# A trace-time planner gets measured durations, and its bisection steps are queued behind regular work

## The chip, the cores and the metric

The kernel runs on 1 core of one Trainium2 chip. The metric is the device time of one execution in microseconds (us). The engines are PE (TensorE matmul; PEld is its weight load), DVE (VectorE), ACT (ScalarE), POOL (GpSimd) and SP (SyncE, which issues the DMAs). Each engine runs its own instruction stream in order; semaphores order the streams against each other.

## The reference

One step of a one-layer hybrid encoder, in float32, for a prompt of 1024 frames and 8 running streams of 16 frames (128 more rows), so 9 tiles of 128 rows; tile 8 is the samples.

```python
h = rmsnorm(x, norm_mix); proj = h @ w_in           # xr, gate, q, k, v, qi, ki, wi
xc, conv_new = causal_conv(xr, conv_prev, conv_w, conv_b)
hs, h_last = rglru(xc, pos, h_prev, ...)            # h = a*h_prev + b, a scan over time
y_a = hs * gelu(gate)
q = rope(rmsnorm(q, q_norm), pos); k = rope(rmsnorm(k, k_norm), pos)
idx_score = sum_heads(relu(qi @ ki.T) * wi)         # -inf outside the 64-frame chunk mask
sel = top_k(idx_score, topk)                        # 256 of up to 1024 keys; 132 of 528 for a sample
y_b = attention of q over the selected k, v only
x = x + concat([y_a, y_b]) @ w_out
x = x + (silu(gate) * up) @ w_ffn_out               # SwiGLU, D_FF = 2816
```

## The kernel before, in words

Every float32 product is made of three matmuls on a high and a low part of each operand (`mm3`, line 243; its matmuls are line 205). The work runs in stages: keys, values and the first norm; the index scores (`index`, line 622); the RG-LRU (`lru_main`, line 1028, four blocks of 128 channels, each in three time pieces of 384 columns); the q projection (`q_tile`, line 1197, two halves of nine tiles); the first half of `W_out` with the rotation of k and the norm of q (`out_tile`, line 1341; `k_rope`; `q_norm`, line 1224, nine POOL multiplications); attention of prompt tiles 0 to 7 and of the eight samples (`attn`, line 1385); the second half of `W_out`; the feed-forward part (`ffn`, line 1623).

**Names.** In the RG-LRU `xp` is the padded input, `xc` the convolved one (ACT copies of PSUM tiles, with the matmuls of line 210 between them), and `tr`, `ti`, `tt` are the gate tiles that DVE turns into the scan over time (`TENSOR_TENSOR_SCAN tr<-tt,ti`). In the q stage `qn` is the normed query and `rp` the POOL part of its rotation; `to` is a small output tile that DVE copies out just as the stage begins. In attention `m` is a head's scores and `mx` its maximum: DVE adds the mask `s` of a tile to the scores in PSUM and takes the maximum in one instruction (printed `ISA m,mx<-ps,s`); ACT makes the exponential and POOL divides; PE transposes `m` (line 215); DVE makes the low part of the result (`rest` and `smr` are buffers for it).

**Top-k by bisection.** The 256th largest score of each row is found bit by bit (`topk`, line 792), in two groups that run beside the stages (line 769, `TK`). Group 0 holds tiles 2 to 5. One of its 32 steps is four ACT instructions over `s` (sign with a sum, `jk<-s,tk_cand`, 384 to 768 columns), then three small DVE updates of `tk_cand`. Group 1 holds tiles 6, 7 and 8. One of its 32 steps (16 on the upper 16 bits, 16 on the lower) is three DVE instructions with a sum over a 16-bit `key` of 896, 1024 and 528 columns (`jk<-key,tk_cnt`, in the first half `jk<-key,tk_cand`), then two or three small updates; such a step is called a pass below. At its end each group makes its masks (`topk_mask`, line 909): a compare, a prefix sum, a second compare with a sum and a third on DVE, and a sum and a scaling of `s` on POOL. Attention of a tile waits for its mask (line 1391), and the samples' part needs tile 8's.

**What sets the order.** All stages are Python generators ("streams"), which `Kernel.run` (line 93) steps while the program is traced. `run` keeps estimates only: `clock`, `pe` (the work handed to PE) and `busy` for each of DVE, ACT and POOL, the time until which that engine has work. Every call of an engine goes through `Metered` (line 36), which adds `fixed + n * each` to `busy`; all such instructions are recorded as line 66. A stream names the time at which it wants to go on. The bisection groups are `side` streams and "fillers" of one engine (line 316: group 0 of ACT, group 1 of DVE): one is stepped when the clock reaches `busy` of its engine less `SLACKS[phase]` (line 103; phases 0 to 4 are index, RG-LRU, q projection, first half of W_out, attention), or in a gap of the estimate of at least `FILL` before a regular instruction (`fill`, line 137). The resulting program is then ordered once more by the framework's scheduler, which follows priorities; `step` (line 155) lowers a filler's priority by 400 places.

Of the kernel before, what the change touches and what calls it, by code (L numbers as in the profile page):

```python
# [11 lines left out]
BF16 = mybir.dt.bfloat16  # L12
I32 = mybir.dt.int32
I16 = mybir.dt.int16
# [21 lines left out]
class Metered:  # L36


    def __init__(self, engine, kernel, name, fixed, each):
        self.engine, self.kernel, self.name, self.fixed, self.each = engine, kernel, name, fixed, each  # L40

    def __getattr__(self, op):
        f = getattr(self.engine, op)
        if op in ("dma_start", "wait", "semaphore") or not callable(f):
            return f

        def call(*args, **kw):
            n = 1
            for a in args:
                if hasattr(a, "shape") and len(a.shape) > 1:  # L50
                    n = max(n, int(np.prod(a.shape[1:])))
            each = self.each
            if self.name == "vector" and op in ("tensor_copy", "tensor_scalar") and "accum_out" not in kw:
                each *= 0.5
            if self.name == "vector" and kw.get("accum_out") is not None and args[1].dtype in (BF16, I16):
                each *= 0.5
            k = self.kernel
            start = k.now() if k.chain is None else k.chain + k.HOP
            k.fill(self.name, start)
            end = max(k.busy[self.name], start) + self.fixed + n * each  # L60
            if self.name == "scalar" and op == "activation":
                end += k.table(args[2])
            k.busy[self.name] = end
            if k.chain is not None:
                k.chain = end
            return f(*args, **kw)  # L66

        return call


class Engines:
    def __init__(self, nc, kernel):
        self.nc = nc
        for name, fixed, each in (("vector", 0.07, 0.00104), ("scalar", 0.2, 0.00072), ("gpsimd", 0.05, 0.0012)):
            kernel.busy[name] = 0.0
            setattr(self, name, Metered(getattr(nc, name), kernel, name, fixed, each))

    def __getattr__(self, x):
        return getattr(self.nc, x)
# [2 lines left out]
class Kernel:  # L82
    def __init__(self, ctx, tc, I, O):
        self.ctx, self.tc, self.I, self.O = ctx, tc, I, O
        self.pe = self.pe0 = 0.0
        self.clock = 0.0
        self.phase = 0
        self.chain = None
        self.busy, self.filler, self.side, self.gap = {}, {}, [], None
        self.nc = Engines(tc.nc, self)  # L90


    def run(self, streams, width, side=(), carry=()):
# [7 lines left out]
        def due(x):  # L101
            e = self.filler.get(x[1])
            return x[0] if e is None else max(x[0], self.busy[e] - self.SLACKS[self.phase])

# [49 lines left out]

    def step(self, g):

        n = self.LATER.get(self.filler.get(g), 0)
        if not n:
            return next(g, None)
        with self.tc.high_priority(offset=-n):  # L160
            return next(g, None)

    def begin(self):

# [27 lines left out]
    TABLES = {"exp": (AF.Exp, AF.Tanh), "sqrt": (AF.Sqrt,), "gelu": (AF.Gelu_apprx_tanh, AF.Tanh), "silu": (AF.Silu,)}  # L192
    SYNC = 0.3
    HOP = 0.1
    SLACKS = (1.5, 1.5, -3.0, -3.0, 1.5)
    QUEUE = 8.0
    AHEAD = 2.0

# [1 line left out]
    def mm(self, out, lhsT, rhs, start, stop):  # L200
        n = 1
        for v in rhs.shape[1:]:
            n *= v
        self.pe += max(n, 256 if lhsT.shape[-1] > 64 else 128) / 2400.0
        self.nc.tensor.matmul(out, lhsT, rhs, start=start, stop=stop)  # L205

    def mm4(self, out, lhsT, rhs, start, stop):
# [1542 lines left out]
```

## Time and profile before

| | us |
|---|---|
| median of 3 runs | 1586.41 (1585.03 to 1586.87) |
| the profiled execution | 1582.82, of which the span is 1580.7 |
| PE busy | 1477.3 (93%) |
| DVE busy | 886.4 (56%) |
| ACT busy | 624.4 (39%) |
| POOL busy | 288.7 (18%) |

Busy time is that of one engine over the whole span; the stages differ widely. The stages lie in the span about so: norm, keys and values to 101 us, index 101 to 193, RG-LRU 193 to 397, q projection 397 to about 463, first half of `W_out` to about 519, attention of tiles 0 to 5 to about 590, of tiles 6, 7 and the samples to about 686, second half of `W_out` to about 755, feed-forward to the end. Neighbouring stages overlap by some microseconds.

### The profile page before, as it was taken

Reading aid. Unit: us, or ns where it says so; the run is one execution under the profiler, and the core shown is the slowest. Engines: PE = TensorE matmul, PEld = TensorE weight load, DVE = VectorE, ACT = ScalarE, POOL = GpSimd, SP = SyncE. Lnnn points to the kernel's source line nnn. Section 1 sums busy time; section 2 is a strip of 40 time slices with the busy share of each in tenths; the row PEclk is TensorE's granted clock in tenths of the full one; section 3 lists DMA queues with packets and bytes.
Section 4 is the critical chain, followed back from the end, with each engine's and each line's share of the span. In section 5 each row is a group of like instructions: output and inputs, shape, how many; then the busy total and the mean of one; then the engine's idle time right before and its main releaser. Section 6 shows DMA issues by size and latency. Waiting matters only on the chain.

```text
span 1580.7 us, 21030 instructions
## 1 busy us (share of the span) xinstructions
PE 1477.3 (93%) x7858; PEld 1335.3 (84%) x7858; DVE 886.4 (56%) x1909; ACT 624.4 (39%) x1484; POOL 288.7 (18%) x433
## 2 busy tenths in 40 slices
PE   6899898875989899999999999999999999999998
PEld 6777676764977688888999999999898989898987
DVE  7656899998676887768424242423333242424143
ACT  5447967867631987755312120202020202121100
POOL 5424223227484444400000000000000000000000
PEclk7999899988999899999999999999999999999999
DMA  7211110100140001120302020202020202111002
GB/s 241 66 32 42 35 29 16 29 14 14 44 156 0 8 14 47 48 67 28 94 14 67 14 75 6 80 1 80 1 80 0 81 18 63 30 51 52 29 1 120
DMA packets 93798, 74.66 MB, mean 47 GB/s; under 512 B 13236, under 2 KB 84532, under 8 KB 93696
## 3 DMA queue, kind: packets, MB, share of 16 engines
q1 hardware_dynamic: 93696, 73.32, 15.5%
q8 instruction: 62, 1.02, 0.3%
q14 instruction: 40, 0.33, 0.1%
HBM read 67.03 MB, written 6.27 MB: 46 GB/s over the span
## 4 chain that ended last, share of the span: by engine, by line
PE 72%; DVE 15%; ACT 5%; POOL 3%; issue 3%; DMA 1%; SPq 0%; POOLq 0%; ACTq 0%; DVEq 0%
PE ps L205 67%; DVE jk L66 7%; PE ps L215 3%; DVE tk_cand L66 2%; ACT jk L66 1%; DVE tr L66 1%; POOL rp L66 1%; PE ps L210 1%; DVE ti L66 1%; POOL qn L66 1%; DVE s L66 1%; ACT qeo L66 1%; ACT m L66 1%; ACT relu L66 0%; DMA tab<-in_rope_dram 0%
## 5 line engine op out<-in xcount | busy, mean ns | idle before, releaser
L205 PE MATMUL ps<-hf,w 128*128 128x384 f32 x2556 | 460.6, 338 | 0.0
L205 PEld LDWEIGHTS ps<-hf,w 128*128 128x128 f32 x2556 | 451.5, 187 | 0.8
L205 PE MATMUL ps<-w,a 128*128 128x512 f32 x999 | 239.1, 390 | 0.0
L66 DVE TENSOR_TENSOR acc<-ps,acc 128x512 f32<-128x512 f32 x234 | 161.3, 690 | 134.4 <-PE ps L205 133.9
L205 PEld LDWEIGHTS ps<-w,a 128*128 128x128 f32 x999 | 187.3, 188 | 40.1
L66 ACT ACTIVATE w<-raw 128x512 fp32r<-128x512 f32 x128 | 77.8, 630 | 303.0 <-PE ps L205 220.9
L66 DVE TENSOR_TENSOR sg<-ps,sg 128x384 f32<-128x384 f32 x66 | 36.7, 557 | 276.4 <-PE ps L205 275.9
L66 DVE TENSOR_TENSOR w<-raw,w 128x512 fp32r<-128x512 f32 x116 | 76.8, 687 | 87.4 <-ACT w L66 87.2
L66 ACT ACTIVATE jk<-s,tk_cand 128x384 bf16<-128x384 f32 (+3 forms) x128 | 99.4, 776 | 61.8 <-DVE tk_cand L66 53.0
L66 ACT ACTIVATE a<-sg 128x384 fp32r<-128x384 f32 x66 | 34.5, 523 | 217.9 <-DVE sg L66 217.9
L205 PE MATMUL ps<-hf,rest 128*128 128x384 f32 x612 | 114.5, 334 | 0.0
L205 PE MATMUL ps<-h,w 128*128 128x384 f32 x576 | 108.7, 347 | 0.5 <-ACT relu L66 0.5
L205 PEld LDWEIGHTS ps<-hf,rest 128*128 128x128 f32 x612 | 106.9, 188 | 0.2
L205 PEld LDWEIGHTS ps<-h,w 128*128 128x128 f32 x576 | 102.3, 190 | 4.7 <-ACT relu L66 0.6
L205 PE MATMUL ps<-w,h 128*128 128x256 f32 (+1 forms) x600 | 94.6, 314 | 0.6 <-DVE to L66 0.6
L205 PE MATMUL ps<-w,rest 128*128 128x512 f32 x324 | 83.0, 406 | 8.2 <-POOL rest L66 8.0
L205 PEld LDWEIGHTS ps<-w,h 128*128 128x128 f32 x600 | 82.2, 188 | 7.3 <-DVE to L66 0.9
L205 PEld LDWEIGHTS ps<-w,rest 128*128 128x128 f32 x324 | 61.3, 194 | 22.7 <-POOL rest L66 8.9
L66 ACT ACTIVATE sg<-ps 128x384 f32<-128x384 f32 x66 | 32.1, 486 | 122.0 <-PE ps L205 122.0
L210 PE MATMUL ps<-xp,taps 128*128 128x384 f32 (+2 forms) x128 | 44.5, 504 | 37.7 <-ACT xp L66 37.7
L210 PEld LDWEIGHTS ps<-xp,taps 128*128 128x128 f32 x128 | 26.7, 231 | 51.7 <-issue 43.8
L66 POOL TENSOR_SCALAR m<-m,mx 128x128 f32<-128x128 f32 (+7 forms) x64 | 47.6, 752 | 68.5 <-DVE mx L66 61.7
(261 smaller groups left out, 2185.2 us busy)
## 6 DMA issues: line engine op xcount, KB each, us to landing
raw<-in_w_ffn_in_dram SPq DMA_DIRECT2D x44, 512.0 KB, 4.9
raw<-in_w_ffn_out_dram SPq DMA_DIRECT2D x22, 512.0 KB, 3.5
raw<-in_w_in_dram SPq DMA_DIRECT2D x16, 512.0 KB, 3.8
out_dram<-acc SPq DMA_DIRECT2D x9, 512.0 KB, 2.6
x<-in_x_prompt_dram SPq DMA_DIRECT2D x8, 512.0 KB
acc<-in_x_prompt_dram SPq DMA_DIRECT2D x8, 512.0 KB, 9.1
tab<-in_rope_dram SPq DMA_DIRECT2D x34, 64.0 KB, 1.8
raw<-in_w_out_dram SPq DMA_DIRECT2D x4, 512.0 KB, 3.5
```

The costliest lines, as they stand in the source:

```text
L66: return f(*args, **kw)
L205: self.nc.tensor.matmul(out, lhsT, rhs, start=start, stop=stop)
L210: self.nc.tensor.matmul(out, lhsT, rhs, start=start, stop=stop)
L215: self.nc.tensor.transpose(out, in_, self.ident[0:n, 0:n])
```

## The change

Three things are changed, all in the planner; no computation is changed, and both programs hold the same instructions of the stages.

1. The estimate of an instruction (`Metered`) becomes a formula by engine, operation, type and place. A pass of group 1 was estimated with half the price per column, since its keys are 16-bit; it now has the full one. The matmul's estimate loses its lower bound.
2. A filler's step is queued behind the regular work: `issued` lists every regular instruction of an engine with the estimated end, and `step` looks for the last one that ends, by the estimate, not later than now; every instruction of the step is ordered behind it (`tc.issue_after`). The lowered priority stays.
3. `SLACKS` becomes 0.5 in all phases. It was 1.5 in index, RG-LRU and attention, and -3.0 in the q projection and the first half of `W_out` (where a step thus came only after 3 us without work).

```diff
@@ class Metered: call
-            each = self.each
-            if self.name == "vector" and op in ("tensor_copy", "tensor_scalar") and "accum_out" not in kw:
-                each *= 0.5
-            if self.name == "vector" and kw.get("accum_out") is not None and args[1].dtype in (BF16, I16):
-                each *= 0.5
             k = self.kernel
             start = k.now() if k.chain is None else k.chain + k.HOP
             k.fill(self.name, start)
-            end = max(k.busy[self.name], start) + self.fixed + n * each
+            end = max(k.busy[self.name], start) + self.cost(op, args, kw)
...
-            return f(*args, **kw)
+            said = f(*args, **kw)
+            if not k.filling:
+                k.issued[self.name].append((end, said.ins))
+            return said
+
+    def cost(self, op, args, kw):
...
+        accum = kw.get("accum_out") is not None or op == "tensor_tensor_reduce"
+        one = op in ("tensor_copy", "tensor_scalar", "memset")
+        if self.name == "scalar":
+            return 0.2 + n * 0.0008 + 0.19 * accum
...
+        if one and not accum:
+            return 0.1 + n * (0.00026 if here and all(a.dtype in (BF16, I16) for a in wide) else 0.00052 if here else 0.00104)
+        return 0.157 + n * 0.00104 + 0.08 * accum + 0.1 * (here and not one)
@@ class Engines
-        for name, fixed, each in (("vector", 0.07, 0.00104), ("scalar", 0.2, 0.00072), ("gpsimd", 0.05, 0.0012)):
+        for name in ("vector", "scalar", "gpsimd"):
@@ class Kernel: step
-        n = self.LATER.get(self.filler.get(g), 0)
-        if not n:
+        e = self.filler.get(g)
+        if e is None:
             return next(g, None)
-        with self.tc.high_priority(offset=-n):
-            return next(g, None)
+        now = self.clock if self.gap is None else self.gap
+        last = next((i for t, i in reversed(self.issued[e]) if t <= now), None)
+        with ExitStack() as st:
+            st.enter_context(self.tc.high_priority(offset=-self.LATER[e]))
+            if last is not None:
+                st.enter_context(self.tc.issue_after(last))
+            self.filling = True
+            lat = next(g, None)
+            self.filling = False
+        return lat
@@ class Kernel
-    SLACKS = (1.5, 1.5, -3.0, -3.0, 1.5)
+    SLACKS = (0.5, 0.5, 0.5, 0.5, 0.5)
@@ mm
-        self.pe += max(n, 256 if lhsT.shape[-1] > 64 else 128) / 2400.0
+        self.pe += n / 2400.0 + 0.0167
```

Where it moves instructions is read from the order in which each program hands its instructions to DVE. (A row is the line, the operation, what is written and read, and the size; a sum into `tk_cnt` is part of the instruction.)

**DVE in the third channel block of the RG-LRU.** Before, from the end of a pass to the first scan of the block:

```order
L66 TENSOR_SCALAR jk_911,tk_cnt<-key,tk_cnt 128x896
L66 TENSOR_SCALAR tk_cand<-tk_cand 128x4
L66 TENSOR_SCALAR jk_911,tk_cnt<-key,tk_cnt 128x1024
L66 TENSOR_TENSOR s_2929<-tt,prm 128x8
L66 TENSOR_TENSOR ti<-ti,tr 128x384 x3
L66 TENSOR_SCALAR jk_911,tk_cnt<-key,tk_cnt 128x528
L66 TENSOR_TENSOR ti<-ti,s_2929 128x8
L66 SCALAR_TENSOR_TENSOR tr<-tt,ti 128x384
```

Now:

```order
L57 TENSOR_SCALAR tk_cand<-tk_cand 128x4
L57 SCALAR_TENSOR_TENSOR tt<-tr,tt 128x384 x3
L57 SCALAR_TENSOR_TENSOR tr<-tt 128x384 x3
L57 TENSOR_TENSOR s_3112<-tt,prm 128x8
L57 TENSOR_TENSOR ti<-ti,tr 128x384 x3
L57 TENSOR_TENSOR ti<-ti,s_3112 128x8
L57 SCALAR_TENSOR_TENSOR tr<-tt,ti 128x384
L57 SCALAR_TENSOR_TENSOR tr<-tt,tr,ti 128x384 x2
```

The pass that stood between the gate work and its scan is gone from there; the block's chain is unbroken, though passes still stand ahead of it. (`tr<-tt,ti` and `tr<-tt,tr,ti` are the scan over time.) In the whole RG-LRU stage 31 passes stand before and 20 now.

**DVE at the start of the q projection.** Before:

```order
L66 COPY to<-ps 36x512
L66 TENSOR_TENSOR qn<-qn,tab 128x256
L66 TENSOR_TENSOR qn<-qn,rp 128x256
L66 TENSOR_TENSOR qn<-qn,tab 128x256
L66 TENSOR_TENSOR qn<-qn,rp 128x256
```

Now, behind the first six rows of the rotation, which read as before:

```order
L57 TENSOR_SCALAR jk_911,tk_cnt<-key,tk_cnt 128x528
L57 TENSOR_TENSOR qn<-qn,tab 128x256
L57 TENSOR_SCALAR tk_cand<-tk_cnt 128x3
L57 TENSOR_TENSOR qn<-qn,rp 128x256
L57 SCALAR_TENSOR_TENSOR tk_cnt<-tk_cand,tk_cnt 128x3
L57 TENSOR_SCALAR jk_911,tk_cnt<-key,tk_cnt 128x896
L57 TENSOR_TENSOR qn<-qn,tab 128x256
L57 TENSOR_SCALAR jk_911,tk_cnt<-key,tk_cnt 128x1024
L57 TENSOR_TENSOR qn<-qn,rp 128x256
```

Before, group 1 was done at this point and group 0 was at its masks; the rotation runs on without a pass. Now 5 passes stand in the q projection and 3 in the first half of `W_out`, and in that half also group 0's last four steps, its threshold and all its masks.

**DVE in attention of tile 4 (two pieces of 320 columns for each head).** Before:

```order
L66 ISA m,mx<-ps,s_890 128x320
L66 ISA mx 128x1
L66 TENSOR_TENSOR rest<-ps,rest 128x512
L66 ISA m,mx<-ps,s_890,mx 128x320
L66 ISA mx 128x1
L66 RECIPROCAL mx<-mx 128x1
L66 TENSOR_TENSOR smr<-ps,smr 128x512
```

Now:

```order
L57 ISA m,mx<-ps,s_890,mx 128x320
L57 ISA mx 128x1
L57 TENSOR_SCALAR jk_911,tk_cnt<-key,tk_cnt 128x896
L57 ISA m,mx<-ps,s_890 128x320
L57 ISA mx 128x1
L57 TENSOR_TENSOR smr<-ps,smr 128x512 x2
L57 TENSOR_SCALAR jk_911,tk_cnt<-key,tk_cnt 128x1024
L57 ISA m,mx<-ps,s_890,mx 128x320
```

Group 1's last four passes stand in attention: two among tiles 0 to 3, two among tiles 4 and 5, followed there by its threshold and the three masks of tiles 6, 7 and 8, which stood in the RG-LRU stage before. PE's matmuls are the same in number and kind.

## Rows read from the trace of the kernel before

**Rows 1.** The page: the span, the busy time of each engine (share of the span, instructions), and DVE's busy tenths in 40 equal slices of the span.

```profile
span 1580.7 us, 21030 instructions
PE 1477.3 (93%) x7858; PEld 1335.3 (84%) x7858; DVE 886.4 (56%) x1909; ACT 624.4 (39%) x1484; POOL 288.7 (18%) x433
DVE  7656899998676887768424242423333242424143
```

**Rows 2.** The view by windows: start and end in us, length, then the busy time of PE, PEld, DVE, ACT and POOL in it (with their instructions), the granted clock of PE, the DMA share and GB/s. In turn: index, RG-LRU with the first microseconds before it, q projection with the first half of W_out, attention of tiles 0 to 5, of it tiles 4 and 5, attention of tiles 6, 7 and the samples, and all that follows the second half of W_out.

```profile
101.00:193.00 92.00, 81.47 (x379) 63.67 (x378) 71.40 (x127) 73.92 (x169) 27.15 (x43) 0.94 0.14 36
187.00:397.00 210.00, 163.53 (x754) 138.87 (x755) 198.24 (x492) 152.87 (x322) 68.98 (x90) 0.91 0.08 22
418.00:519.00 101.00, 89.25 (x507) 77.61 (x508) 65.94 (x120) 39.70 (x205) 67.90 (x85) 0.94 0.25 81
518.00:590.00 72.00, 66.03 (x373) 55.73 (x374) 63.17 (x221) 62.48 (x150) 28.70 (x46) 0.93 0.03 8
555.00:590.00 35.00, 33.34 (x203) 28.31 (x201) 30.59 (x100) 27.83 (x59) 13.36 (x16) 1.00 0.05 16
590.00:686.00 96.00, 92.24 (x605) 81.25 (x604) 72.21 (x194) 68.63 (x172) 41.27 (x48) 0.96 0.14 39
755.00:1581.00 826.00, 821.28 (x4316) 772.14 (x4313) 290.59 (x460) 141.01 (x263) 0.00 (x0) 1.00 0.15 45
```

**Rows 3.** The chain of waits, share of the stretch by engine, tile and line: first of the RG-LRU (187 to 418 us), then of attention (518 to 686 us).

```profile
by line: DVE jk L66 44.9%; DVE tk_cand L66 11.6%; DVE tr L66 9.6%; ACT jk L66 6.9%; DVE ti L66 4.8%; issue 3.5%; DVE tt L66 3.2%; DVE key L66 2.5%; DVE tk_cnt L66 2.0%; ACT L66 1.7%; DVE s L66 1.4%; ACT tr L66 1.2%; ACT relu L66 1.0%; ACT t
by line: PE ps L205 56.5%; PE ps L215 20.8%; ACT m L66 4.8%; PE ps L1569 3.2%; ACT qeo L66 2.5%; issue 2.2%; ACT rest L66 1.7%; DVE m L66 1.6%; DVE qeo L66 1.3%; ACT yF L66 1.1%; ACT smr L66 1.0%; ACT smp L66 0.8%; POOL smp L66 0.5%; DVE re
```

**Rows 4.** DVE's groups by form in 192 to 416 us: operation, written and read tiles, size and type, count, busy us and mean ns of one, idle time before. The three instructions of a pass in its second half, the three updates after a step of group 0, then the four of the mask of the 1024-column tile.

```profile
L66 DVE TENSOR_SCALAR_CACHE_REDUCE jk<-key,tk_cnt 128x896 bf16<-128x896 int16 x16 | 18.3, 1144 | 0.4
L66 DVE TENSOR_SCALAR_CACHE_REDUCE jk<-key,tk_cnt 128x1024 bf16<-128x1024 int16 x16 | 20.5, 1278 | 0.4
L66 DVE TENSOR_SCALAR_CACHE_REDUCE jk<-key,tk_cnt 128x528 bf16<-128x528 int16 x16 | 12.2, 760 | 0.3
...
L66 DVE SCALAR_TENSOR_TENSOR tk_cand<-tk_cnt 128x4 int32<-128x4 f32 x26 | 8.8, 338 | 3.7 <-ACT jk L66 3.6
L66 DVE SCALAR_TENSOR_TENSOR tk_cand<-tk_cand 128x4 int32<-128x4 int32 x26 | 7.8, 299 | 0.1
...
L66 DVE TENSOR_SCALAR tk_cand<-tk_cand 128x4 int32<-128x4 int32 x24 | 6.2, 259 | 0.1
...
L66 DVE TENSOR_SCALAR jk<-s,tk_cnt 128x1024 bf16<-128x1024 f32 x1 | 1.0, 994 | 0.0
L66 DVE TENSOR_TENSOR_SCAN key<-jk 128x1024 int16<-128x1024 bf16 x1 | 2.3, 2277 | 0.0
L66 DVE TENSOR_SCALAR_CACHE_REDUCE s<-s,tk_cnt 128x1024 f32<-128x1024 f32 x1 | 1.2, 1247 | 0.0
L66 DVE SCALAR_TENSOR_TENSOR jk<-key,tk_cnt,jk 128x1024 bf16<-128x1024 int16 x1 | 1.3, 1252 | 0.0
```

**Rows 5.** DVE's timeline (start us, length us, instruction) in 293 to 298 us: the first instruction of two passes in a row.

```profile
293.48 1.15 DVE L66 TENSOR_SCALAR_CACHE_REDUCE jk<-key,tk_cnt 128x896 bf16<-128x896 int16 x1
...
297.20 1.15 DVE L66 TENSOR_SCALAR_CACHE_REDUCE jk<-key,tk_cnt 128x896 bf16<-128x896 int16 x1
```

**Rows 6.** ACT's groups by form in 192 to 416 us (columns as in rows 4; behind the last bar also what ended the idle time before): the four instructions of a step of group 0, and the reading of their sums.

```profile
L66 ACT ACTIVATE jk<-s,tk_cand 128x768 bf16<-128x768 f32 x26 | 24.2, 932 | 0.5
L66 ACT ACTIVATE jk<-s,tk_cand 128x640 bf16<-128x640 f32 x26 | 21.4, 825 | 0.5
L66 ACT ACTIVATE jk<-s,tk_cand 128x512 bf16<-128x512 f32 x26 | 18.7, 718 | 0.5
L66 ACT ACTIVATE jk<-s,tk_cand 128x384 bf16<-128x384 f32 x26 | 16.1, 618 | 53.7 <-DVE tk_cand L66 48.3 <-DVE ti L66 3.6 <-DVE tk_cnt L66 1.9
L66 ACT ACTIVATION_READ_ACCUMULATOR jk<-s,tk_cand 128x1 f32 x104 | 19.8, 190 | 0.0
```

**Rows 7.** The view of waits in 190 to 420 us: the waiting group, its releaser, us waited in all, number of waits, longest wait. First PE, then ACT.

```profile
PE ps L210 <- ACT xp L66: 37.7, 9, 8.9
ACT jk L66 <- DVE tk_cand L66: 48.3, 18, 5.6
```

**Rows 8.** Timelines (start, length, engine, instruction, in brackets the idle time before and its releaser) between 417 and 518 us: DVE as the q projection begins, the last POOL multiplications of `qn`, the matmuls of `W_out` and of attention that wait.

```profile
417.62 0.68 DVE L66 COPY to<-ps 36x512 f32<-36x512 f32 x1 [0.25 <-DMA gq<-in_q_norm_dram]
423.38 0.67 DVE L66 TENSOR_TENSOR qn<-qn,tab 128x256 f32<-128x256 f32 x1 [5.08 <-ACT sq L66]
...
466.01 9.98 POOL L66 TENSOR_TENSOR qn<-qn,qss 128x512 f32<-128x512 f32 x9 [1.60 <-DVE qss L66]
...
477.26 2.93 PE L205 MATMUL ps<-w,rest 128*128 128x512 f32 x6 [4.33 <-POOL rest L66]
...
517.36 0.44 PE L205 MATMUL ps<-k,qeo 128*128 128x128 f32 x2 [2.98 <-DVE qeo L66]
```

**Rows 9.** POOL's groups by form: the sum that ends a mask, of the 1024-column tile (380 to 412 us) and of a 512-column one (415 to 480 us).

```profile
L66 POOL TENSOR_TENSOR s<-s,jk 128x1024 f32<-128x1024 f32 x1 | 3.6, 3582 | 0.0
L66 POOL TENSOR_TENSOR s<-s,jk 128x512 f32<-128x512 f32 x1 | 1.2, 1157 | 0.0
```

More of the change, by code (lines that the diff above doesn't have):

```diff
@@ L36, with __init__ @@
 class Metered:
-    def __init__(self, engine, kernel, name, fixed, each):
-        self.engine, self.kernel, self.name, self.fixed, self.each = engine, kernel, name, fixed, each
+    def __init__(self, engine, kernel, name):
+        self.engine, self.kernel, self.name = engine, kernel, name
     def __getattr__(self, op):
@@ L47, in call @@
         def call(*args, **kw):
[L48 to L51, printed above, removed]
-            each = self.each
-            if self.name == "vector" and op in ("tensor_copy", "tensor_scalar") and "accum_out" not in kw:
-                each *= 0.5
-            if self.name == "vector" and kw.get("accum_out") is not None and args[1].dtype in (BF16, I16):
-                each *= 0.5
             k = self.kernel
@@ L65, in call @@
                 k.chain = end
-            return f(*args, **kw)
-        return call
+            said = f(*args, **kw)
+            if not k.filling:
+                k.issued[self.name].append((end, said.ins))
+            return said
+        return call
+    def cost(self, op, args, kw):
+        tensors = [a for a in args if hasattr(a, "shape") and len(a.shape) > 1]
+        n = max([1] + [int(np.prod(a.shape[1:])) for a in tensors])
+        wide = [a for a in tensors if int(np.prod(a.shape[1:])) == n]
+        here = all(a.space == bass.MemoryType.SB for a in wide)
+        accum = kw.get("accum_out") is not None or op == "tensor_tensor_reduce"
+        one = op in ("tensor_copy", "tensor_scalar", "memset")
+        if self.name == "scalar":
+            return 0.2 + n * 0.0008 + 0.19 * accum
+        if self.name == "gpsimd":
+            return 0.1 + n * 0.0011 if one else 0.2 + n * 0.0023
+        if op == "tensor_tensor_scan":
+            return 0.2 + n * 0.0022
+        if one and not accum:
+            return 0.1 + n * (0.00026 if here and all(a.dtype in (BF16, I16) for a in wide) else 0.00052 if here else 0.00104)
+        return 0.157 + n * 0.00104 + 0.08 * accum + 0.1 * (here and not one)
 class Engines:
@@ L73, in __init__ @@
         self.nc = nc
-        for name, fixed, each in (("vector", 0.07, 0.00104), ("scalar", 0.2, 0.00072), ("gpsimd", 0.05, 0.0012)):
+        for name in ("vector", "scalar", "gpsimd"):
             kernel.busy[name] = 0.0
-            setattr(self, name, Metered(getattr(nc, name), kernel, name, fixed, each))
+            kernel.issued[name] = []
+            setattr(self, name, Metered(getattr(nc, name), kernel, name))
     def __getattr__(self, x):
@@ L89, in __init__ @@
         self.busy, self.filler, self.side, self.gap = {}, {}, [], None
+        self.issued, self.filling = {}, False
         self.nc = Engines(tc.nc, self)
```

## The prediction

> **What bounds the kernel now.** Read first the page's head: PE is busy 93% of the span and DVE 56% [rows 1]. That average hides where time is left, so DVE's slices come next: 7 to 9 tenths in the first 18 of 40 slices, 2 to 4 behind them [rows 1]. The windows then give one stage at a time [rows 2]. From 755 us on PE is busy 821.3 of 826.0 us: half of the time has nothing to win, and the change does not touch its instructions. In the RG-LRU (187 to 397) DVE is busy 198.2 of 210 us and PE only 163.5. From 418 to 519 PE has 89.2 of 101 and DVE 65.9; in attention of tiles 0 to 5 PE has 66.0 of 72 and DVE 63.2.
>
> The chain of waits says the same [rows 3]: 44.9% of the RG-LRU stretch are DVE passes over `key` (`jk`) and 11.6% the small updates `tk_cand`, while attention's chain is PE (56.5% and 20.8%). So the passes bound the RG-LRU today, and later stages have little DVE work of the bisection in them. The waits name the victims [rows 7]: PE waits 37.7 us for `xp`, an ACT copy, and ACT waits 48.3 us for `tk_cand`, the update that stands in DVE's queue behind passes. ACT runs in order, so `xp` stands behind a sign that waits for DVE.
>
> **The change part by part.** No work goes or comes; it is moved. The counts are from the order of each program, the durations from this trace. A pass takes 3.72 us from start to start [rows 5], of which its three large instructions are 1.14 + 1.28 + 0.76 = 3.18 [rows 4]. The doubled estimate and the wait for regular work move group 1 to later stages: 32 passes stand before as 1 in the index and 31 in the RG-LRU; now 20 are in the RG-LRU, 5 in the q projection, 3 in the first half of W_out, 4 in attention. The masks of tiles 6 to 8 go from the RG-LRU to attention: the four large instructions for 1024 columns take 0.99 + 2.28 + 1.25 + 1.25 = 5.77 us [rows 4], by 2448/1024 columns 13.8, with the small ones about 14.5.
>
> *Index: -4.* Group 0 has two steps fewer here. A step is 0.93 + 0.82 + 0.72 + 0.62 + 4 x 0.19 = 3.85 us of ACT [rows 6], so 7.7 in all. No engine fills this stage (PE 81.5, ACT 73.9, DVE 71.4 of 92 [rows 2]), so the bounds are 0 and -7.7; I take the middle.
>
> *RG-LRU: -33.* DVE loses 11 x 3.72 = 40.9 us of passes, 14.5 of masks and about 5 of the end of group 0, 60 in all. What is late next? PE's own 163.5 us is one end: a gain of 46. ACT is the other: 152.9 us [rows 2] less two steps, 145.2, plus the time in which it waits for its updates. Alone these take 0.34 + 0.30 + 0.26 = 0.90 us [rows 4]; for 24 steps that is 21.6, together 166.8. Two engines that hand work back and forth are never quite full; DVE today fills 198.2/210 = 94% of this stage, and 166.8/0.944 = 177. The gain is 210 - 177 = 33. If the updates still stand behind passes, the wait per step stays at 53.7/26 = 2.07 us [rows 6], and 145.2 + 24 x 2.07 = 195: a gain of 15. I take 33, since the order shows the blocks' gate work in one piece before the scan, with a pass less between; both ends stay in the range.
>
> *q projection and first half of W_out: +14.* DVE has 65.9 us here [rows 2]. To these come 8 x 3.72 = 29.8 of passes and 8.6 of group 0 (four updates of 0.90 and about 5 of its threshold), 104.3 against a wall of 101. The rotation of `qn` now shares DVE with passes, and what follows hangs on it: POOL's multiplications (9.98 us), `W_out`'s matmuls that wait 4.33 us for POOL, attention's first that wait 2.98 [rows 8]. At the start DVE waits 5.08 us for the first tile's sums [rows 8]; passes can cover some of it, and I leave 3. Fully packed the stage is 107 us (+7 with rounding). At 85% full it is 123 (+22). At 93%, a point under the RG-LRU's own, since three engines hand `qn` on, 112 + 3 = 115: +14. Cover is not to be had from PE: it has 89.2 of 101 already.
>
> *Attention of tiles 0 to 5: +28.* DVE has 63.2 of 72 [rows 2]. Four passes are 14.9, the masks 14.5, and 2.9 us of regular work come forward from the next stage: 95.5. That work lightens the next stage, so the wall to compare with is 72 + 3 = 75. Packed: 95.5, +20.5. At the 88% that DVE has here today (63.2/72): 109, +34. At 93%: 103, +28. PE sets the end here today; DVE's 95.5 is far past PE's 66.0, so the bound changes hands. A pass stands right ahead of an `m,mx` instruction, for which ACT, POOL and then the transposes wait; each of them comes up to 1.28 us later.
>
> A mask's prefix sum and last compare read two tiles of SBUF. In tiles 4 and 5 POOL is busy 13.4 of 35 us [rows 2], dividing `m`. The trace shows what such a meeting might cost: the sum that ends a mask took POOL 3.58 us for 1024 columns, against 1.16 for 512, so 3.1 times for twice the work [rows 9]. By the smaller row the 1024 would be 2.3, and the excess is 1.3 us. The Trainium skill (SBUF — State Buffer, "Who interferes with whom") says that a DVE instruction with two SBUF inputs contends with a GpSimd instruction that reads SBUF, and that whoever issues first blocks the other for the whole instruction; one with at most one SBUF input, outside its fast modes, does not. By that rule the passes are harmless to POOL, which no row here contradicts, and the moved masks are not: (2.28 + 1.25) x 2448/1024 = 8.4 us of DVE could each hold POOL up, and if all of it reached the end, attention would be +36. Rows 2 leave POOL 21 us free in that window, so I add nothing.
>
> *Tiles 6 and 7, samples, the rest: 0.* DVE has 72.2 of 96 there and about 2 less now; PE, 92.2, sets the end [rows 2]. The matmul's estimate and the new slack act only through the order counted above.
>
> *Sum:* -4 - 33 + 14 + 28 = +5 on the profiled execution's 1582.82 (span 1580.7 and 2.1 around it), so 1588. The median of the runs shown is 1586.41, 3.6 above; by it the time is 1591.
>
> **The rivals.**
>
> *PE takes over early, and the time falls.* The place is the RG-LRU. If ACT's updates come at once and gate work is never behind a pass, the stage ends at PE's 163.5 us (-46), and in attention passes fall into DVE's holes while PE works, so that it packs (+20.5); q and W_out cost +7 to +14. With the index's -4 the sum is -15 to -23, so about 1568, in a band of 1558 to 1580. It decides from the point where the RG-LRU is shorter than 173 us with attention under 98. For it: PE waits 37.7 us for `xp` alone [rows 7], all due to bisection. Against it: ACT's own sum with the shortest updates is 166.8, above PE's.
>
> *ACT's wait stays, and the time rises.* The planner still thinks in estimates; a step of group 0 needs an update on DVE, and such an update is now queued behind regular work too. Then the RG-LRU gains 15 instead of 33, and the sum is -4 - 15 + 14 + 28 = +23: 1609, in a band of 1598 to 1615. For it: 48.3 us of ACT's waiting [rows 7] came with updates already near in the order. Against it: a third of the passes that stood in the way is gone.
>
> *The change doesn't do what it says.* If the orders differ only where engines wait anyway, all terms are nought and the time stays at 1586. Against it: 60 us of DVE work changes stage, out of one where DVE bounds.
>
> **How the numbers follow.** 0.2% is 3.2 us, about what a measurement of this kernel can tell from no change. My forecast, 1591, has 0.45; its own range, with one of the later terms (+7 to +22, +20.5 to +34) at an end, is 1583 to 1599. Of that I count 0.03 as faster, 0.17 as within 0.2% and 0.25 as slower. The early PE has 0.30, all faster; ACT's wait 0.22, all slower; no effect 0.03, same. So faster 0.33, same 0.20, slower 0.47. The range to hold 8 of 10 leaves out a tenth at each end: it reaches into the first rival to 1565 and into the second to 1609.
>
> **What would show each step.** In the profile after, the windows give the RG-LRU's length: 177 us right, 195 the second rival, under 170 the first. The wait of `xp` should fall from 37.7 to under 15, and that of ACT's first sign for `tk_cand` to about 1 us per step. From the end of the RG-LRU to the first attention matmul the stretch should grow by 14 with DVE over 90% busy; attention of tiles 0 to 5 by 28, its chain no longer PE's but DVE's, with `jk` and the masks in it. From 590 us on, in today's count, nothing should change beyond 2 us. I am wrong if PE stays the chain of attention in spite of 32 us more DVE work, or if the RG-LRU's gain is not the largest term but one of them is of the other sign.

## The result and the profile after

The changed kernel takes 1605.6 us (median of 4, 1603.69 to 1607.6) against 1586.64 of the kernel before: the ratio is 1.0122, 95% interval 1.0104 to 1.0139, so about 19 us slower. The profiled executions differ by a little more, spans 1602.9 and 1580.7, and the stages below add up to these 22.2 us, but for rounding.

The page of the kernel after; the lines answer to [rows 1]:

```profile
span 1602.9 us, 21013 instructions
PE 1486.5 (93%) x7858; PEld 1341.0 (84%) x7858; DVE 891.4 (56%) x1909; ACT 625.3 (39%) x1482; POOL 287.0 (18%) x433
DVE  7656777777998997857614152424233332424243
```

The same work, then: as many instructions on PE, DVE and POOL and two fewer on ACT, with the busy times of DVE, ACT and POOL within 5 us of [rows 1]; PE's is 9 us longer. DVE's slices are lower in the RG-LRU (7 where 8 and 9 stood) and higher behind it.

The view by windows of the kernel after, cut where its own stages begin, columns as in [rows 2]. In turn: RG-LRU, q projection, first half of `W_out`, attention of tiles 0 to 5, then up to the last score and up to the feed-forward part; last, the RG-LRU from 187 us, as in [rows 2].

```profile
207.00:369.30 162.30, 137.39 (x651) 116.16 (x650) 127.59 (x311) 122.69 (x261) 54.56 (x81) 0.94 0.09 24
369.30:423.10 53.80, 52.39 (x438) 51.82 (x437) 45.20 (x91) 36.55 (x184) 33.68 (x47) 0.99 0.31 104
423.10:499.30 76.20, 56.50 (x235) 43.93 (x233) 70.02 (x166) 27.69 (x78) 40.12 (x47) 0.90 0.10 31
499.30:606.70 107.40, 80.48 (x396) 65.45 (x397) 97.95 (x284) 68.55 (x161) 40.54 (x55) 0.85 0.03 8
606.70:681.00 74.30, 70.30 (x461) 61.91 (x461) 57.20 (x160) 55.25 (x133) 33.00 (x40) 0.98 0.16 44
681.00:767.50 86.50, 80.74 (x422) 67.02 (x421) 57.89 (x124) 41.29 (x90) 5.46 (x6) 0.96 0.17 47
187.00:369.30 182.30, 157.39 (x763) 135.58 (x762) 137.82 (x347) 142.05 (x304) 55.63 (x84) 0.95 0.09 25
```

A stage is taken here from its first matmul to that of the next: RG-LRU from the first product with `xp`, then the first of the q projection, of `W_out`, of attention; attention of tiles 0 to 5 ends at DVE's first instruction of the samples, and the next stretch at the first matmul of the feed-forward part. By these marks, in us:

| | before | after | difference | forecast |
|---|---|---|---|---|
| up to the RG-LRU | 206.3 | 207.1 | +0.8 | -4 |
| RG-LRU | 190.2 | 162.2 | -28.0 | -33 |
| q projection | 53.0 | 53.8 | +0.8 | |
| first half of `W_out` | 67.8 | 76.2 | +8.4 | with the line above +14 |
| attention of tiles 0 to 5 | 72.6 | 107.4 | +34.8 | +28 |
| on to the feed-forward part | 155.7 | 160.8 | +5.1 | 0 |
| feed-forward part | 835.0 | 835.4 | +0.4 | 0 |

By these marks the trace has 28 passes in the RG-LRU before and 17 after, and after it 6 in the q projection, 5 in the first half of `W_out` and 4 in attention. (The counts ahead of the result are from the order of the program: 31 and 20, 5, 3 and 4. DVE runs some passes a stage later than that.)

The gain in the RG-LRU came, and more than that was given back. The chain of waits of the kernel after, shares by tile and line, first of 190 to 369 us, then of attention, 499 to 607; they answer to [rows 3]. The third line is the kernel before over tiles 0 to 5 alone, 518 to 590 us, since [rows 3] goes on to 686:

```profile
by line: DVE jk L57 23.1%; ACT jk L57 14.5%; PE ps L227 9.4%; DVE tk_cand L57 8.2%; PE ps L232 6.9%; DVE tr L57 5.5%; issue 4.6%; DVE ti L57 4.5%; ACT L57 4.3%; ACT tr L57 4.1%; DVE key L57 2.6%; DVE sp_p L57 2.3%; ACT taps L57 1.9%; ACT yF
by line: PE ps L227 22.8%; issue 13.1%; DVE m L57 12.7%; DVE jk L57 10.2%; PE ps L237 6.7%; DVE qeo L57 4.9%; ACT m L57 4.8%; DVE smr L57 3.8%; DVE key L57 3.7%; DVE rest L57 3.1%; DVE s L57 2.8%; DVE k L57 2.2%; POOL s L57 1.7%; DVE mx L57
by line: PE ps L205 44.9%; PE ps L215 19.5%; ACT m L66 8.7%; ACT qeo L66 5.8%; ACT rest L66 4.0%; issue 3.9%; DVE m L66 3.8%; DVE qeo L66 3.1%; ACT yF L66 1.6%; DVE rest L66 0.9%; DVE mx L66 0.9%; DVE smr L66 0.9%; ACT smr L66 0.8%; DVE k L
```

Passes (`DVE jk`) fell from 44.9% to 23.1% of the RG-LRU's chain. The chain of tiles 0 to 5 was PE's at 64%, with about 10% for DVE, and is now mixed: PE has 30% and DVE, by its tiles `m`, `jk`, `qeo`, `smr`, `key`, `rest` and `s`, 41%. The waits in 190 to 369 us (ACT, then PE) answer to [rows 7]:

```profile
ACT jk L57 <- DVE tk_cand L57: 32.5, 12, 7.1
PE ps L232 <- ACT xp L57: 16.3, 7, 6.1
```

PE's wait for `xp` went from 37.7 us to 16.3, 21 us less in a stage that is 28 shorter.

### The profile page after: what moved, and what is told of

Same layout as the page of the kernel before. It is cut to its first block, busy times and chain, and to the rows that moved or that the text cites. A ratio compares the mean times of both kernels' runs of the same rounds, so it can differ in the third digit from the quotient of the medians.

```text
span 1602.9 us, 21013 instructions
## 1 busy us (share of the span) xinstructions
PE 1486.5 (93%) x7858; PEld 1341.0 (84%) x7858; DVE 891.4 (56%) x1909; ACT 625.3 (39%) x1482; POOL 287.0 (18%) x433
## 3 DMA queue, kind: packets, MB, share of 16 engines
q8 instruction: 62, 1.02, 0.3%
## 4 chain that ended last, share of the span: by engine, by line
PE 72%; DVE 16%; ACT 5%; issue 4%; DMA 2%; POOL 1%; SPq 0%; ACTq 0%; DVEq 0%; POOLq 0%
PE ps L227 67%; DVE jk L57 5%; PE ps L237 3%; ACT jk L57 2%; PE ps L232 2%; DVE m L57 1%; DVE tk_cand L57 1%; DVE tr L57 1%; DVE ti L57 1%; DVE s L57 1%; DVE key L57 1%; ACT tr L57 1%; DMA raw<-in_w_out_dram 1%; ACT L57 1%; DVE acc L57 0%
## 5 line engine op out<-in xcount | busy, mean ns | idle before, releaser
L57 ACT ACTIVATE jk<-s,tk_cand 128x384 bf16<-128x384 f32 (+3 forms) x128 | 99.2, 775 | 52.4 <-DVE tk_cand L57 37.8
L227 PE MATMUL ps<-smr,vhl 128*128 128x512 f32 x162 | 54.0, 426 | 8.5 <-ACT smr L57 6.5
L227 PE MATMUL ps<-k,qeo 128*128 128x384 f32 (+5 forms) x192 | 53.8, 389 | 6.0 <-DVE qeo L57 4.4
```

The lines of the kernel that those rows point to most:

```text
L57: said = f(*args, **kw)
```

## The experiments

Three theories were set up first. A: the time follows the stage in which the bisection's DVE work stands. B: the ordering behind regular work costs by itself. C: the new estimates misplan the regular work, apart from the bisection. The lengths of the stages are by the marks above; medians are compared with the kernel before measured on the same chip, and the ratio has its 95% interval. The lengths are those of the profiled execution; that of e2 was the longest of its ten, 1589.06 us.

| run | median us | ratio to before | RG-LRU | q | half of `W_out` | attention 0-5 | on to feed-forward |
|---|---|---|---|---|---|---|---|
| after | 1605.6 | 1.0122 (1.0104-1.0139) | 162.2 | 53.8 | 76.2 | 107.4 | 160.8 |
| e1 | 1603.09 | 1.0107 (1.0092-1.0122) | 191.0 | 53.6 | 69.4 | 84.1 | 159.2 |
| e2 | 1584.24 | 0.9991 (0.9981-1.0) | 189.3 | 56.6 | 67.0 | 74.6 | 155.3 |
| e3 | 1598.44 | 1.0082 (1.0067-1.0097) | 168.3 | 55.7 | 89.2 | 78.1 | 164.8 |
| e4 | 1607.06 | 1.0131 (1.0114-1.0148) | 168.8 | 53.0 | 92.9 | 84.2 | 164.4 |
| e5 | 1589.38 | 1.0029 (1.0019-1.004) | 193.8 | 52.0 | 74.2 | 71.8 | 157.0 |
| e6 | 1614.67 | 1.0185 (1.017-1.02) | 192.7 | 53.6 | 68.8 | 100.3 | 156.7 |
| e7 | 1582.79 | 0.9986 (0.9976-0.9995) | 186.8 | 53.3 | 67.7 | 73.3 | 161.5 |
| e8 | 1587.17 | 1.0013 (1.0001-1.0024) | 189.3 | 53.3 | 74.0 | 71.5 | 157.9 |
| e9 | 1603.7 | 1.0119 (1.0102-1.0136) | 165.3 | 53.9 | 76.6 | 102.0 | 162.4 |
| e10 | 1601.03 | 1.0102 (1.0087-1.0117) | 168.3 | 55.7 | 89.7 | 77.9 | 164.1 |
| e11 | 1592.33 | 1.0046 (1.0031-1.0061) | 168.1 | 55.7 | 89.2 | 73.1 | 159.5 |
| e12 | 1606.9 | 1.0134 (1.0117-1.0151) | 174.6 | 72.7 | 82.6 | 72.3 | 161.1 |

**e1: the change without the ordering.**

```diff
             st.enter_context(self.tc.high_priority(offset=-self.LATER[e]))
-            if last is not None:
-                st.enter_context(self.tc.issue_after(last))
```

> The changed kernel with the ordering behind regular work taken out; estimates and slacks stay changed. Its DVE order has 2 passes in the index stage, 30 in the RG-LRU and all masks of tiles 6 to 8 there, none later. Theory A (the time follows the stage in which the bisection's DVE work stands: in attention of tiles 0 to 5 it adds in full, 35 us for 32; in the RG-LRU about 28 us for 60; in the q projection nothing): attention of tiles 0 to 5 back at 73 us, RG-LRU back at about 190, time 1586 within 6. Theory B (the ordering itself costs, wherever the passes stand): 1586 as well, since it is gone. Theory C (the new estimates misplan the regular work): still slow, 1597 or more.

The bisection is back in the RG-LRU, which takes 191.0 us, and the time is still 1603.09. A is not enough and B fails with it, for both said 1586; of the three only C fits: attention takes 84.1 us without a single pass in it. (This run keeps the new slacks too, which were never run alone; e6 below has the old ones.) Its window:

```profile
524.40:608.50 84.10, 70.15 (x391) 60.42 (x391) 68.34 (x228) 67.02 (x159) 31.23 (x49) 0.88 0.04 10
```

No engine is near full there; PE has 70.2 of 84.1 us.

**e2: the ordering alone, with the old estimates and slacks.** In the kernel before:

```diff
+        last = next((i for t, i in reversed(self.issued[e]) if t <= now), None)
...
+            if last is not None:
+                st.enter_context(self.tc.issue_after(last))
```

> The kernel before with the ordering behind regular work alone; old estimates, slacks and matmul price. Its DVE order has all 32 passes and the three masks in the RG-LRU. Theory A: attention at 73 us, RG-LRU about 190 (the same 210 us of DVE work as before), time 1586 within 6. Theory B: the ordering's cost stays, 1598 or more. Theory C: 1586, the estimates being the old ones.

1584.24 us, the same as before or a trifle less. B falls. The ordering also moves nothing to later stages unless the estimates do: none of the 32 passes stands behind the RG-LRU.

**e3: a pass at half the price per column again, all else as changed.**

```diff
-        return 0.157 + n * 0.00104 + 0.08 * accum + 0.1 * (here and not one)
+        half = kw.get("accum_out") is not None and args[1].dtype in (BF16, I16)
+        return 0.157 + n * (0.00052 if half else 0.00104) + 0.08 * accum + 0.1 * (here and not one)
```

> The changed kernel in which an instruction with a sum over 16-bit data is again estimated with half the price per column, as before. Its DVE order has 28 passes in the RG-LRU and 4 in the q projection, the masks of tiles 6 to 8 in the q projection and the first half of W_out, nothing in attention. Theory A: RG-LRU 162 + 0.47 x 9 x 3.72 = 178 us, q projection 54, first half of W_out about 76, attention 73: 1605.6 + 16 - 34 = 1587, within 1582 to 1592. Theory B: about 1600, since the ordering is unchanged. Theory C: about 1600, all other estimates being the new ones.

1598.44 us, near what B and C expected. A's figures fail in detail: the RG-LRU is shorter than expected (168.3, not 178) though it holds 25 passes by the marks, 8 more than the changed kernel's 17, and the half of `W_out` is longer (89.2, not 76). The waits there (429 to 518 us):

```profile
PE ps L228 <- POOL rest L57: 25.7, 6, 12.2
POOL s L57 <- DVE jk L57: 18.1, 5, 4.9
ACT jk L57 <- DVE tk_cand L57: 16.8, 3, 7.9
```

PE waits for POOL's low parts of `W_out`, and POOL stands at sums of masks that wait for DVE. That is one reading; e10 tries it.

**e4: the change with the old slacks.**

```diff
-    SLACKS = (0.5, 0.5, 0.5, 0.5, 0.5)
+    SLACKS = (1.5, 1.5, -3.0, -3.0, 1.5)
```

> The changed kernel with the old SLACKS (1.5, 1.5, -3, -3, 1.5). Its DVE order has 23 passes in the RG-LRU, 6 in the q projection, 3 in the first half of W_out, the masks of tiles 6 and 7 there and that of tile 8 at the start of attention. Theory A: RG-LRU 162 + 0.47 x 4 x 3.72 = 169 us, q projection 54, first half of W_out about 79, attention 76: 1605.6 + 7 + 3 - 31 = 1585, within 1579 to 1591. Theory B or C: about 1600, since ordering and estimates are unchanged.

1607.06 us: A fails again. As in e3, no pass stands in attention (tile 8's mask does), the RG-LRU is short (168.8), and the half of `W_out` (92.9) and attention (84.2) take the gain back.

**e5 to e8: one group of estimates at a time, in the kernel before.** Here S says that one estimate carries the loss of e1, and N that any new set of numbers does.

e5 has the matmul's price:

```diff
-        self.pe += max(n, 256 if lhsT.shape[-1] > 64 else 128) / 2400.0
+        self.pe += n / 2400.0 + 0.0167
```

e6 has the new table for DVE, e7 for ACT and e8 for POOL, and for the other engines the old numbers (`cost0`); in e6:

```diff
+        if self.name not in ('vector',):
+            return self.cost0(op, args, kw)
```

> The kernel before with the new matmul estimate alone. With theories A and B fallen, what is asked is which estimate makes the regular work slower by the 17 us of the run without the ordering. Theory S (one estimate carries it): three of these four runs at 1586 within 4, one near 1603. Theory N (no estimate is the culprit; any new set of numbers lands on another order of the regular work, and the order before was a good one): each of the four is 4 to 15 us slower, and their sum is well over 17. By S, the matmul estimate is my second guess: 1586 or 1603. By N: 1590 to 1600.

> The kernel before with the new DVE estimates alone, no ordering behind regular work, old slacks. By S this is my first guess for the culprit, since the score instruction with its maximum goes up by 0.17 us and all waits of attention are planned behind it: 1603, with attention of tiles 0 to 5 at about 84 us instead of 73. By N: 1590 to 1600.

> The kernel before with the new ACT estimates alone (0.08 ns a column more, and 0.19 us for a sum), no ordering, old slacks. By S: 1586 within 4. By N: 1590 to 1600.

> The kernel before with the new POOL estimates alone (a two-operand instruction of 512 columns goes from 0.66 to 1.38 us), no ordering, old slacks. By S: 1586 within 4. By N: 1590 to 1600.

S holds, in that one estimate stands out: the DVE estimates alone cost 29 us (1614.67, where 1603 was expected, and 100.3 us of attention where 84 was), the matmul's 4, POOL's 2, and ACT's save 2 to 3 (0.9986, 0.9976 to 0.9995, the only run whose interval lies below 1 in full). They do not add: the four together, in e1 and with the new slacks, lose 17. Their sum, 32, is well over 17, as N had it, but three of the four are under N's 4 us. In e6 the same instructions run from attention's first matmul to the feed-forward part in 256.9 us instead of 228.3. That stretch in the kernel before, then in e6:

```profile
517.40:745.70 228.30, 218.20 (x1273) 186.77 (x1274) 182.93 (x511) 164.14 (x383) 69.97 (x94) 0.96 0.13 35
```

```profile
521.00:777.90 256.90, 226.78 (x1275) 194.18 (x1276) 185.47 (x510) 165.14 (x383) 69.70 (x94) 0.92 0.12 32
```

DVE has no more to do (185.5 against 182.9 us). PE is idle 30.1 us instead of 10.1, and its own matmuls take 8.6 us more at a granted clock of 0.92 instead of 0.96. The waits of PE in this stretch of e6 are many and short:

```profile
PE ps L239 <- ACT rest L57: 7.2, 5, 2.4
PE ps L1603 <- POOL kn L57: 6.9, 2, 3.5
PE ps L239 <- ACT smr L57: 4.3, 4, 1.4
PE ps L239 <- DVE qeo L57: 3.7, 2, 3.3
PE ps L249 <- POOL m L57: 3.7, 2, 2.3
```

No engine is late as a whole: PE arrives at a product before its operand. What differs is the order in which the streams' work was handed out, since an estimate touches nothing else. Read as a list, the 1276 matmuls that e6's trace has here hold 872 in an order common with the kernel before; e8's hold 1236 of 1272, and e2's 1270. And yet the new DVE numbers are nearer to the trace: a masked maximum over 320 columns takes 0.48 to 0.55 us and 0.08 for its result, the new estimate is 0.157 + 320 x 0.00104 + 0.08 = 0.57, the old 0.07 + 0.333 = 0.40; a low part of 512 columns takes 0.68, estimated 0.69 now and 0.60 before. Which DVE estimate it is was not tried.

**e9: the old DVE estimates from attention on.**

```diff
+        if self.name == "vector" and self.kernel.phase == 4:
+            return self.cost0(op, args, kw)
```

> The changed kernel in which DVE instructions are estimated with the old numbers from attention on (phase 4), and with the new ones before. Its DVE order has the same 19 passes in the RG-LRU, 5 in the q projection, 4 in the first half of W_out and 4 in attention, and the three masks in attention. Theory S (the new DVE estimates make the planner hand out attention's regular work in a worse order; without any bisection there it took 15 us more from the first attention matmul to the feed-forward part): that stretch falls from 268 to about 253 us, time 1590 within 6. Rival (the queue of passes and masks is all of attention's loss): 265 or more, time 1602 or more.

1603.7 us: the rival holds, but for a stretch a trifle under its 265 us. With passes and masks in attention, the old estimates are worth little: from its first matmul to the feed-forward part 264.4 us instead of 268.2. The windows of e9, tiles 0 to 4 with part of 5, the last 18 us, and both, then a piece of PE's timeline:

```profile
501.70:586.00 84.30, 68.37 (x349) 54.10 (x350) 78.52 (x241) 59.51 (x144) 30.30 (x45) 0.89 0.03 8
586.00:603.70 17.70, 2.29 (x13) 1.87 (x12) 13.78 (x30) 4.60 (x9) 11.80 (x9) 0.59 0.04 12
501.70:603.70 102.00, 70.66 (x360) 55.97 (x361) 92.30 (x270) 64.11 (x153) 42.09 (x53) 0.83 0.03 9
```

```profile
602.57 0.40 PE L241 MATMUL ps<-jk,key 128*128 128x264 bf16 x1 [15.41 <-DVE jk L57]
```

In this order PE ran ahead of DVE until it met the one matmul that needs the sample tile's finished mask, and stood 15.4 us with all that was queued behind.

**e10: e3 with the last two instructions of a mask on DVE.**

```diff
-        self.pool_tt(s, s, eq, ALU.add)
-        nc.gpsimd.tensor_scalar(s, s, BIG, -BIG, op0=ALU.mult, op1=ALU.add)
+        nc.vector.tensor_tensor(s, s, eq, op=ALU.add)
+        nc.vector.tensor_scalar(s, s, BIG, -BIG, op0=ALU.mult, op1=ALU.add)
```

> The run with the half price for a pass (28 passes in the RG-LRU, 4 in the q projection, masks in the q projection and the first half of W_out, where that half took 89 us instead of 68) with the two last instructions of a mask, a sum and a scaling, on DVE instead of POOL. Theory P (POOL runs in order and stands 18 us at sums of masks that wait for DVE, with the low parts of W_out and the rotation of q queued behind, and PE waits 25.7 us for them): PE's wait for POOL's rest under 12 us, the half at 78 us or less, time 1587 within 5. Rival (DVE's own queue sets that stretch): DVE gets about 5 us more work, the half at 89 or more, time 1598 or more.

1601.03 us, not better than e3. P falls, and the rival's figures came (the half at 89 or more, time 1598 or more): POOL's wait at the masks is gone, and PE's for POOL's `rest` is 16.9 us where under 12 was named. PE's waits for `rest` in all (431 to 521 us), then, from the timelines, ACT's longest wait, POOL's `qn`, PE's second wait and POOL's longest:

```profile
PE ps L228 <- POOL rest L57: 16.9, 2, 8.9
```

```profile
455.58 0.62 ACT L57 ACTIVATE jk<-s,tk_cand 128x384 bf16<-128x384 f32 x1 [17.76 <-DVE tk_cand L57]
...
460.32 11.44 POOL L57 TENSOR_TENSOR qn<-qn,qss 128x512 f32<-128x512 f32 x8 [2.04 <-DVE qss L57]
...
473.04 2.93 PE L228 MATMUL ps<-w,rest 128*128 128x512 f32 x6 [8.90 <-POOL rest L57]
...
504.30 1.30 POOL L57 TENSOR_TENSOR rest<-yF,rest 128x512 fp32r<-128x512 f32 x1 [15.37 <-ACT rest L57]
```

A sign of group 0 held ACT up for 17.8 us, for an update in DVE's queue. The product at 473.04 needs a `rest` that stood behind eight multiplications of `qn` on POOL, and these had waited for `qss` on DVE. POOL's wait of 15.4 us ends later, at 504.3; there the copy on ACT stood behind one of `k` that waits 12.9 us for DVE. DVE is busy 85.6 of these 89.7 us. So POOL was a link, at a different place each time; that DVE's queue sets the whole stretch fits all of these waits and was not tried by itself.

**e11: e10 with e9's edit as well.**

```diff
+        if self.name == "vector" and self.kernel.phase == 4:
+            return self.cost0(op, args, kw)
...
+        nc.vector.tensor_tensor(s, s, eq, op=ALU.add)
```

> The run before it with the old DVE estimates from attention on as well. Theory S and P together: RG-LRU about 168 us, first half of W_out 78, from the first attention matmul to the feed-forward part 230 instead of 243: time 1575 within 7, faster than both kernels. If only S holds, 1586; if only P holds, 1587; if neither, 1598 or more.

1592.33 us. Without bisection in attention the old DVE estimates are worth 9 us (1.0046 against 1.0102): attention 73.1 instead of 77.9 and 159.5 instead of 164.1 behind it. S holds, P does not, though 1586 is missed by 6.

**e12: e9 with slacks of 2.5 before attention.** Both groups are then done before attention.

```diff
-    SLACKS = (0.5, 0.5, 0.5, 0.5, 0.5)
+    SLACKS = (2.5, 2.5, 2.5, 2.5, 0.5)
```

> The changed kernel with the old DVE estimates from attention on and SLACKS of 2.5 in the four stages before it. Its DVE order has 23 passes in the RG-LRU with the whole end of group 0 there, 6 passes in the q projection and 3 in the first half of W_out, with the masks of tiles 6 to 8 behind the last rotation of q there; attention has no bisection. If place decides (passes are free under the q projection, cost little in the first half of W_out as long as they stand behind the rotation of q, and cost all their length in attention) and the old DVE estimates give attention its old order: RG-LRU about 172 us, q projection 54, first half of W_out about 77, attention to the feed-forward part about 232: 1586 - 18 + 1 + 9 + 4 = 1582, within 1575 to 1589, faster than both kernels. If any DVE work of the bisection in the first half of W_out costs as in the runs with the half price and the old slacks (21 to 25 us): 1594 or more.

1606.9 us, a miss: 1582 was expected, and 1594 or more if all such work costs in the half of `W_out`. Attention is as before:

```profile
536.70:609.00 72.30, 65.35 (x372) 55.56 (x373) 63.16 (x214) 60.99 (x148) 27.60 (x45) 0.92 0.03 8
```

But group 0's masks now stand on DVE in the last block of the RG-LRU. ACT waits 20.62 us for DVE's `tr` there, and PE, which has begun the q projection, waits for a mask's instruction (its operands `w` and `h` have no part in masks, but group 0's prefix sums lie in PSUM tiles, so it probably waits for one to come free) and then for the tail of the scan (timelines of ACT, then PE):

```profile
406.62 1.28 ACT L57 ACT_TABLE_LOAD   x1 [20.62 <-DVE tr L57]
```

```profile
397.60 13.58 PE L241 MATMUL ps<-w,h 128*128 128x256 f32 x96 [8.53 <-DVE jk L57]
...
418.08 0.37 PE L251 MATMUL ps<-ident,tail 128*36 128x128 f32 x1 [6.57 <-DVE tail L57]
```

The q projection took 72.7 us, 19.7 more, and the half of `W_out` 14.8 more. No version tried beats the kernel before by more than e7's 0.14%.

## Why the prediction was right, and where it was wrong

The time lies in the range of 1565 to 1609 and on the side that had the most weight, slower. The 1591 is 15 us short, and the time is outside the likeliest case's own 1583 to 1599. That the range holds it is in part luck. Its upper end came from the second rival, whose 1609 is nearer by accident: that rival's mechanism, an RG-LRU that gains only 15, did not occur.

- *RG-LRU: -33 forecast, -28.0.* The mechanism held. From 187 us on, where the prediction's window begins, the stage took 182 us, against 177 forecast and 195 of the second rival. PE's wait for `xp` fell to 16.3 (under 15 was named). ACT's for `tk_cand` was 32.5 us where 21.6 was taken, 0.90 for each of 24 steps; with ACT's busy 142.1 us it makes 174.6 of the 182.3. The term was mis-sized by 5, and this wait, 11 us over, is the likely reason; it was not tried apart.
- *q projection and first half of `W_out`: +14 forecast, +9.2.* DVE got 34 us of work, near the 38.4 reckoned (it is 89% busy over the two; over 90% was named), but the place counts. By the windows of the kernel before, q projection and half of `W_out`, below, the q projection took 10.8 of them, with six passes, for 0.8 us: PE has 52.4 of 53.8 there, and ACT, not DVE, frees its PSUM. The half of `W_out` took 23.3 for 8.4 us. I had set the two stages' DVE sum against one wall; the first hides its share.

```profile
396.60:449.60 53.00, 52.04 (x439) 51.50 (x438) 34.43 (x62) 33.85 (x179) 33.25 (x47) 1.00 0.31 102
449.60:517.40 67.80, 56.78 (x239) 45.25 (x238) 46.77 (x96) 15.82 (x51) 39.92 (x47) 0.92 0.13 41
```

- *Attention of tiles 0 to 5: +28 forecast, +34.8.* That DVE's queue takes over from PE is shown. The clean pair is e9 and e12, with the same estimates in attention: 92.3 us of DVE work in 102.0, and 63.2 in 72.3, so 29.7 us of time for 29.1 of work. The stage came to 107.4 us where 103 was reckoned, with 98.0 us of DVE work instead of 95.5, and DVE 91% full instead of 93%; the 3 us that the forecast took off again, for work pulled out of the next stage, did not come back there.
- *Index: -4 forecast, +0.8; behind attention: 0 forecast, +5.1.* These are the misses that I had no step for.

The step that failed is "the matmul's estimate and the new slack act only through the order counted above". I counted where passes, steps and masks went and took the regular work's order as it was. The estimates rule that too. e1 shows the size, 17 us with the bisection where it had been, and e6 the source, the DVE numbers. In the changed kernel the DVE estimates from attention on cost less: with the old ones e9 has 4 us back of the 40 that are lost between attention's first matmul and the feed-forward part. That is a net figure and no bound, for e9's order brought the wait of 15.4 us with it, and the estimates of the other engines stayed new. What makes the 5 us behind attention was not isolated; e7 (161.5) and e9 (162.4) have it too, under different estimates.

The question of POOL under the moved masks is answered in part. POOL waits 8.5 us at the sum of tile 6's mask in attention. Of these groups of the kernel after (540 to 607 us) only the compare is longer than in [rows 4]:

```profile
L57 DVE TENSOR_SCALAR jk<-s,tk_cnt 128x1024 bf16<-128x1024 f32 x1 | 1.5, 1493 | 0.0
...
L57 DVE TENSOR_TENSOR_SCAN key<-jk 128x1024 int16<-128x1024 bf16 x1 | 2.3, 2294 | 0.0
...
L57 DVE TENSOR_SCALAR_CACHE_REDUCE jk<-key,tk_cnt 128x1024 bf16<-128x1024 int16 x2 | 2.5, 1264 | 0.0
```

The passes kept their length (1264 ns, 1278 before), as did the scan (2294, 2277), and the compare went from 994 to 1493. The Trainium skill (SBUF — State Buffer, "Who interferes with whom") names such a compare as one that can take the shared ports, and a pass, which also writes a sum, as one that can't: the trace agrees with both. One of the two passes ran beside a division on POOL, and neither was longer for it. The compare of 896 columns took 0.69 us beside an idle POOL before and 1.12 in attention, where a division had 0.64 us left as it began. But the one of 528 went from 1.30 down to 0.67, so the move to attention does not lengthen it as such. By the same section of the Trainium skill the scan, with its two inputs in SBUF, can collide too: the scan above tests nothing, since POOL stood idle beside it, but in the kernel before one collision is plain, and it is POOL that pays:

```profile
355.02 2.02 DVE L66 TENSOR_TENSOR_SCAN key<-jk 128x896 int16<-128x896 bf16 x1
355.07 1.96 POOL L66 TENSOR_SCALAR xp<-xp 128x3 f32<-128x3 f32 x1 [14.18 <-ACT xp L66]
```

A copy of three columns, 0.20 us in the median of its eight, started just behind the scan and ended with it. In attention little of this was left: two of the three scans met an idle POOL, and the sum of 1024 columns, whose 3.58 us in [rows 9] gave the prediction its excess of 1.3, took 2.15. I had added nothing for all this: DVE's sum in attention came to 98.0 us, where 95.5 was reckoned, and what of the 2.5 is POOL's doing was not measured apart.

## What to carry to other kernels

A table of costs in a planner moves all work that it orders: count the regular rows too, and run the table alone, without the feature that came with it. Truer costs are no better plan as such; here the DVE estimates nearer to the trace lost 29 us, and a change of them is an experiment for each engine by itself. Side work moved out of a bound stage was nearly free here where another engine was full in its stead and nothing else waited for its engine: six passes beside a full PE cost 0.8 us, and 29 us of passes and masks beside a DVE at 87% cost 30.

## What the runs showed of the hardware that was not expected

The stretch that left PE idle for longer paid again in PE's own time. From attention's first matmul to the feed-forward part the same products take 218.2 us of PE in the kernel before, at a mean granted clock of 0.96, and 231.5 in the one after:

```profile
499.30:767.50 268.20, 231.52 (x1275) 194.38 (x1276) 213.03 (x564) 165.09 (x384) 79.00 (x100) 0.92 0.11 31
```

So 13 of the 40 us lost there are busy time; the two clocks alone, 0.96 to 0.92, would make about 9 of them if every product slowed in proportion, an estimate. Within it the granted clock is 0.85 over tiles 0 to 5, where PE was busy 80.5 of 107.4 us, against 0.93 in [rows 2]; both are means between the two levels of 1.2 and 2.4 GHz. In the last 18 us of e9's attention, where PE was busy 2.3 us, it is 0.59, close to the lower one.
